# A two-block transformer step on one core: deferred uses of turned tiles, and token-major state-space channels

## The chip, the cores and the metric

The program runs on one core of one Trainium2 chip. The time is the device time of one launch in microseconds (us); three runs of the kernel before gave 1686.46, 1687.34 and 1688.99 us, median 1687.34.

## The reference, cut to what matters

256 tokens of width 1024 go through two blocks. The first block has two layers. Each layer is a feed-forward network (SwiGLU), a mixer, and a second feed-forward network. The second block has one mixer of another kind, one cross-attention and one feed-forward network, which the change reaches only through the feed-forward network's helper. The mixer of a layer of the first block is

```python
uv, c_q, c_kv, k_rope, z, xbc, dt_raw, gates = jnp.split(h @ w_in[l], IN_OFFSETS, axis=-1)
y_a = gmlp_mixer(uv, ...)                      # gelu, norm, a 128x128 matrix over tokens, product
y_b = mla_mixer(c_q, c_kv, k_rope, ...)        # low-rank heads, rope, causal attention
y_c = ssd_mixer(z, xbc, dt_raw, ...)           # xbc: causal conv of width 4 over tokens, silu, then the scan
g = jax.nn.sigmoid(gates).reshape(bsz, s, N_BRANCH, D_MODEL)
merged = (g[:, :, 0] * (y_a @ w_branch[l, 0]) + g[:, :, 1] * (y_b @ w_branch[l, 1])
          + g[:, :, 2] * (y_c @ w_branch[l, 2]))
x = x + merged @ w_out[l]
```

`xbc` has 1024 channels: 512 are the scan's inputs, 512 its two state projections. The convolution runs along tokens, one channel at a time.

## The kernel before, in words

**Products.** All weights are float32. `wload` (L158) brings a tile of 128x1024 weights from memory into a ring `stage` of 5, ScalarE casts it to the ring `whi` of 4 (L165), and VectorE writes the rest of the split, `wlo`, also 4 deep (L166). Each product of 128 x 128 x n is then three matmuls, high by high, high by low and low by high (`mac`, L288; they show as L290, L291 and L292). With 512 columns a weight tile holds two of the eight 128-row pieces of the width, and both 128-token tiles use it: 2 x 2 x 3 = 12 matmuls for a tile. The slot of weight tile i is free again when the last matmul of tile i-4 is done.

**Two directions.** `lin_tok` (L294) gives token-major results: activations are the stationary operand, 512 weight columns the moving one. `lin_ft` (L313) gives channel-major results (channels on partitions): 128 weight columns are stationary, and the 256 tokens move. The mixer's `xbc` uses `lin_ft`, since the convolution wants tokens along the free axis.

**Turning a tile.** A token-major result that feeds a product has to be turned. `to_T` (L258) does it with TensorE transposes into PSUM, then `split_evac` (L187: a cast on ScalarE, a subtraction on VectorE). `flip_T` (L282) does it without TensorE: `flip` (L267) has VectorE transpose 32x32 blocks into a tile `flip` (L273), SyncE writes it to memory `flips` in four pieces (L277), and reads it back as `flipped` (L279); `split_evac` follows. The channels then stand in another order, so the weight rows behind are permuted on the host (`_flipped`). `flipped` has one buffer.

**Order.** The mixer's steps come in the order of a list,

```python
SEQ = "x u q z S A g0 b0 g2 g1 b2 b1"
```

x: the state-space channels and their convolution; u: the gated MLP up to its turned output `yaT`; q: heads; z: the state-space gate; S: the scan, output `ycT`; A: attention, output `ybT`; g0, g1, g2: gate projections; b0, b1, b2: the branch products of `yaT`, `ybT`, `ycT`. After the last branch the merged rows `mg` are transposed to `mh`, `ml` for the product with `w_out`. Within these, the tile framework fixes each engine's order of instructions when the program is built, by priorities (weights and the chains S and A stand higher) and by what its own schedule has ready; on the chip each engine then works through its list in that order. SyncE issues all transfers, weights and turned tiles alike, from one list.

Of the kernel before, what the change touches and what calls it, by code (L numbers as in the profile page):

```python
# [16 lines left out]
P = 128  # L17
# [14 lines left out]
BUFS = dict(  # L32
    sg=2, hb=1, flip=2, flipped=1,
    cg=2, xb=2, gv=2, gu=2, sq=2, q=2, k=2, kv=4, xs=2, xd=2, y=2, yo=2, jk=2, pr=2, pT0=2, pT1=2, ao=2, L=2, cbm=2, rp=2,
    D1=2, Mb=2, pm=2, XT=2, X=3, s5m0=2, s5x0=2, s5t=4, sq2=2, tg=1, o2=1, vn=2)
SEQ = "x u q z S A g0 b0 g2 g1 b2 b1"
NS, NW = 5, 4
COLS = ((0, 512), (512, 512))
LAST = ((0, 512), (512, 256), (768, 256))
# [27 lines left out]
class Net:  # L67
    def __init__(self, ctx, tc, a, outs):
        self.tc, self.nc, self.a, self.outs = tc, tc.nc, a, outs
        mk = lambda n, b=None, **k: ctx.enter_context(tc.tile_pool(name=n, bufs=b, **k))  # L70
        self.big = mk("big")
        self.sma, self.small = None, {}
        self.junk = mk("junk", 1)
        self.ps = mk("ps", space=PSUM)
        self.dram = mk("dram", 2, space=bass.MemoryType.DRAM)
        self.lane = ""
        self.wdma, self.ahead = [], []
# [73 lines left out]
    def _shape(t, shape):  # L151
# [4 lines left out]
        return t.rearrange("p (a b c) -> p a b c", b=shape[1], c=shape[2])  # L156

    def wload(self, src, shape):  # L158
        nc = self.nc
        n = int(np.prod(shape))  # L160
        i = len(self.wdma)
        with self.tc.high_priority(WPRIO):
            s, h, l = [ring[:, i % ring.shape[1], :n] for ring in (self.stage, self.whi, self.wlo)]
            self.wdma.append(self.dma(s, src, 4))
            nc.scalar.copy(h, s)  # L165
            self.wsub = nc.vector.tensor_tensor(l, s, h.bitcast(F32), ALU.subtract).ins  # L166
        return self._shape(h, shape), self._shape(l, shape)
# [98 lines left out]

    def flip(self, src, w, rows=4):  # L267


        nc = self.nc  # L270
        n = rows * w
        r = self.A([512], "flip")[:, :n]
        nc.vector.transpose(r, src)  # L273
        d = self.dram.tile([P, 512], F32, name="flips", tag="flips")[:32 * rows, :4 * w]
        to = d.rearrange("(j c) (i e) -> i c j e", c=32, e=w)
        for i in range(4):
            nc.sync.dma_start(out=to[i], in_=r[i * 32:i * 32 + 32].rearrange("p (j e) -> p j e", e=w))  # L277
        raw = self.A([512], "flipped")[:32 * rows, :4 * w]
        nc.sync.dma_start(out=raw, in_=d)  # L279
        return raw.rearrange("p (a k b) -> p a k b", a=4, b=32)  # L280

    def flip_T(self, src, n, hi, lo, t):  # L282

        tok = slice(t * P, (t + 1) * P)
        hi, lo = [z[:, :, tok].rearrange("p k (a b) -> p k a b", b=32) for z in (hi, lo)]
        self.split_evac(self.flip(src, n * 32).rearrange("p a k b -> p k a b"), hi, lo)

# [25 lines left out]
    def lin_ft(self, xT, w, c, out):  # L313
# [186 lines left out]
    def mixer1(self, l, norm, nxt):  # L500
        nc, a = self.nc, self.a
        v, act, pe = nc.vector, nc.scalar, nc.tensor
        tt, stt, ts = v.tensor_tensor, v.scalar_tensor_tensor, v.tensor_scalar
        lay = self.lay = Arena(self, 3072, "lay1")
        xT, r = norm["xT"], norm["r"]
# [58 lines left out]

        xc, qkv, zs = [], [], []

        def channels():

            rrow = self.r_rows(r, lay)
            for g in range(2):  # L570
                xb = self.A([4, S], "xb")
                for c2 in range(2):
                    p = self.mm()
                    for c in range(2):
                        self.lin_ft(xT, self.wcols(a["m1_xbc"][l][g * 4 + c2 * 2 + c][None], P), 0, p[:, c * S:(c + 1) * S])
                    tt(xb[:, c2 * 2:c2 * 2 + 2], self._shape(p, [2, S]),
                       rrow[:, None, :].to_broadcast([P, 2, S]), ALU.mult)
                d = self.A([4, S], "xc")
# [22 lines left out]
        def heads():  # L601
# [3 lines left out]
            for hf in range(2):  # L605
# [4 lines left out]
                for t in range(2):  # L610
                    p, pk = pqs[t], pks[t]
                    with self.tc.high_priority(EPRIO):
# [47 lines left out]
        def ssd():  # L660
# [18 lines left out]
            for t in range(2):  # L679
# [134 lines left out]
        for step in SEQ.split():  # L814
            i = int(step[1:] or 0)
            if step[0] == "b":
                branch(i, ys[i], not begun)
# [676 lines left out]
def _prep(inp):  # L1494
# [117 lines left out]
```

## Time and profile before

| | us |
|---|---|
| median of 3 runs | 1687.34 |
| the profiled execution's own time | 1684.87 |
| its span, first to last instruction | 1683.2 |
| TensorE busy in it | 1653.3 (98%) |
| VectorE busy | 1152.4 (68%) |
| ScalarE busy | 904.5 (54%) |
| mean granted TensorE clock | 0.996 of 2.4 GHz |

Matmuls are pipelined: one of 512 columns lasts 391 ns by itself, and the next starts long before it ends. What one costs is the distance between two starts, so the timeline is the view to read it from, not the busy time. The mixer of layer one runs from about 196 to 416 us, that of layer two from about 799 to 1018 us.

### The profile page before, as it was taken

How to read it: one execution, taken by the hardware profiler on the slowest of the kernel's cores; microseconds unless marked ns; L12 is line 12 of the kernel's file. 1: busy time of each engine (PE TensorE's matmuls, PEld its weight loads, DVE VectorE, ACT ScalarE, POOL GpSimd, SP SyncE). 2: the span in 40 equal slices, each digit the busy share in tenths (PEclk: the TensorE clock that was granted, in tenths of full speed). 3: DMA queues.
4: the chain of work that ended last, by engine and by line, in shares of the span. 5: the costliest groups of instructions: out<-in, count | busy, mean ns of one | idle time of the engine just before them, and what ended most of it. 6: DMA issues, size and time to landing. Idle time of an engine off the chain costs nothing.

```text
span 1683.2 us, 24727 instructions
## 1 busy us (share of the span) xinstructions
PE 1653.3 (98%) x9090; PEld 1412.7 (84%) x9090; DVE 1152.4 (68%) x1904; ACT 904.5 (54%) x1361; POOL 80.7 (5%) x73
## 2 busy tenths in 40 slices
PE   8999999998999999999999989999999999999998
PEld 6888898887888888888988877888899888888888
DVE  5665599756666556665897666799689746756664
ACT  5444476663545444444676645545477555654443
POOL 0000013000000000000121000000010100000000
PEclk9999999999999999999999999999999999999999
DMA  7777577753687757776777645767764224347872
GB/s 258 242 239 246 178 225 235 225 179 122 193 252 249 230 176 237 248 242 184 230 232 232 191 147 188 225 211 235 230 196 144 64 63 154 123 151 246 260 234 98
DMA packets 158986, 337.15 MB, mean 200 GB/s; under 512 B 35984, under 2 KB 76432, under 8 KB 158864
## 3 DMA queue, kind: packets, MB, share of 16 engines
q1 hardware_dynamic: 158864, 335.57, 63.6%
q8 instruction: 71, 1.16, 0.3%
q14 instruction: 51, 0.42, 0.1%
HBM read 312.43 MB, written 23.07 MB: 199 GB/s over the span
## 4 chain that ended last, share of the span: by engine, by line
PE 95%; DVE 1%; ACT 1%; DMA 1%; issue 0%; SPq 0%; POOL 0%; POOLq 0%; DVEq 0%; ACTq 0%
PE mm L290 28%; PE mm L291 28%; PE mm L292 28%; PE tp L206 1%; PE mmm L290 1%; PE mmm L292 1%; PE mmm L291 1%; PE ch L758 1%; PE chs L1005 1%; PE ch L780 1%; PE ch L1143 0%; PE ch L721 0%; ACT whi L165 0%; PE tp L773 0%; PE ch L1138 0%
## 5 line engine op out<-in xcount | busy, mean ns | idle before, releaser
L166 DVE TENSOR_TENSOR wlo<-stage,whi 128x1024 fp32r<-128x1024 f32 (+3 forms) x552 | 659.6, 1199 | 331.6 <-ACT whi L165 313.1
L165 ACT CAST whi<-stage 128x1024 fp32r<-128x1024 f32 (+3 forms) x552 | 568.4, 1035 | 445.1 <-PE mm L292 366.0
L291 PE MATMUL mm<-wlo,xh 128*128 128x512 f32 (+3 forms) x1264 | 484.2, 385 | 0.0
L292 PE MATMUL mm<-whi,xl 128*128 128x512 f32 (+4 forms) x1264 | 481.0, 385 | 0.0
L290 PE MATMUL mm<-whi,xh 128*128 128x512 f32 (+3 forms) x1264 | 468.1, 385 | 0.1
L291 PEld LDWEIGHTS mm<-wlo,xh 128*128 128x128 f32 x1264 | 237.8, 188 | 45.7 <-DVE wlo L166 0.2
L290 PEld LDWEIGHTS mm<-whi,xh 128*128 128x128 f32 x1264 | 237.0, 188 | 45.9 <-ACT xh L210 0.5
L292 PEld LDWEIGHTS mm<-whi,xl 128*128 128x128 f32 x1264 | 236.8, 188 | 44.8
L292 PE MATMUL mm<-whi,hTl 128*128 128x512 f32 (+1 forms) x484 | 179.0, 370 | 0.0
L291 PE MATMUL mm<-wlo,hTh 128*128 128x512 f32 (+1 forms) x484 | 179.0, 370 | 0.0
L290 PE MATMUL mm<-whi,hTh 128*128 128x512 f32 (+1 forms) x484 | 178.8, 371 | 0.0
L174 POOL TENSOR_TENSOR small<-small,cst 128x1 f32<-128x1 f32 (+2 forms) x60 | 62.1, 1043 | 1154.1 <-DVE small L172 1110.1
L188 ACT CAST hTh<-flipped 128x512 fp32r<-128x512 f32 (+1 forms) x60 | 35.2, 587 | 132.5 <-DMA flipped<-flips 130.9
L292 PEld LDWEIGHTS mm<-whi,hTl 128*128 128x128 f32 x484 | 91.2, 188 | 15.5
L290 PEld LDWEIGHTS mm<-whi,hTh 128*128 128x128 f32 x484 | 91.2, 189 | 15.3
L291 PEld LDWEIGHTS mm<-wlo,hTh 128*128 128x128 f32 x484 | 91.3, 189 | 15.2
L189 DVE TENSOR_TENSOR hTl<-flipped,hTh 128x512 fp32r<-128x512 f32 (+1 forms) x60 | 38.8, 647 | 79.5 <-ACT hTh L188 75.3
L291 PE MATMUL mm<-xl,whi 128*128 128x256 f32 x320 | 90.7, 284 | 1.1 <-DVE xl L211 1.1
L290 PE MATMUL mm<-xh,whi 128*128 128x256 f32 x320 | 90.3, 284 | 1.2 <-ACT xh L210 1.2
L292 PE MATMUL mm<-xh,wlo 128*128 128x256 f32 x320 | 90.2, 283 | 0.0
L291 PEld LDWEIGHTS mm<-xl,whi 128*128 128x128 f32 x320 | 61.3, 192 | 1.6 <-DVE xl L211 1.5
L290 PEld LDWEIGHTS mm<-xh,whi 128*128 128x128 f32 x320 | 61.2, 192 | 1.4 <-ACT xh L210 1.4
(519 smaller groups left out, 2004.2 us busy)
## 6 DMA issues: line engine op xcount, KB each, us to landing
stage<-in_ffn_in SPq DMA_DIRECT2D x176, 512.0 KB, 4.3
stage<-in_ffn_out SPq DMA_DIRECT2D x88, 512.0 KB, 4.4
stage<-in_m_g SPq DMA_DIRECT2D x48, 512.0 KB, 4.6
stage<-in_f_in SPq DMA_DIRECT2D x44, 512.0 KB, 4.4
flips<-flip SPq DMA_DIRECT2D x232, 64.0 KB, 3.2
flipped<-flips SPq DMA_DIRECT2D x58, 256.0 KB, 3.6
stage<-in_m_br SPq DMA_DIRECT2D x24, 512.0 KB, 4.6
stage<-in_m_out SPq DMA_DIRECT2D x24, 512.0 KB, 3.6
```

Of the source, the lines that this page charges most:

```text
L165: nc.scalar.copy(h, s)
L166: self.wsub = nc.vector.tensor_tensor(l, s, h.bitcast(F32), ALU.subtract).ins
L174: nc.gpsimd.tensor_tensor(r, m, self.mhalf[:, :n], ALU.pow)
L188: self.nc.scalar.copy(hi, ps)
L189: self.nc.vector.tensor_tensor(lo, ps, hi.bitcast(F32), ALU.subtract)
L206: nc.tensor.transpose(p[:, k, t * P:(t + 1) * P], x[t][:, (k0 + k) * P:(k0 + k + 1) * P], self.ident)
L290: mm(out, lh, rh, start=first, stop=False)
L291: mm(out, lh, rl, start=False, stop=False)
L292: mm(out, ll, rh, start=False, stop=last)
L758: pe.matmul(p3[:, i], qT[:96, b * hb + i, toks[t]], kT[:96, b * hb + i, :nk], start=True, stop=True)
L780: pe.matmul(p[:, h * 64:(h + 1) * 64], pT[kb][:, h], vv[kb][:, h], start=kb == 0, stop=kb == t)
L1005: pe.matmul(q, self.s5bc[ct][:, 2 * (E5 - 1 - e) + i], um[:, :, e], start=e == 0, stop=e == E5 - 1)
```

## The change

There are four parts.

1. **Deferred uses.** `flip` no longer reads back at once. It puts two things on a list: the read of `flipped`, due 5 weight tiles later or more, and the use (the ScalarE cast and what follows), due 3 weight tiles after that. `wload` runs what is due before it loads the next tile, and orders it behind the last weight tile's transfer and cast. `flipped` has two buffers. `FLUSH` names steps in front of which what an earlier step has put on the list is run at once: b0 flushes u's, A flushes q's, q flushes what stands ahead of the steps, c flushes x's. All feed-forward networks use `flip_T` and so follow the new rule.
2. **Channels.** `xbc` is projected token-major with 512 columns (`lin_flip`), scaled on ScalarE, turned by `flip`, and copied by ScalarE into `xb`. The row of scales across channels (`r_rows`, two transposes) and the scaling on VectorE (four instructions of 128x512 a mixer) go. The convolution is a step of its own, c.
3. **Attention and scan outputs** are turned by `to_T` instead of `flip_T`: 2 x 4 transposes for `ycT` and 4 x 2 for `ybT` a mixer.
4. **Order.** z comes before q, S before g0, A behind g0.

```diff
+FLUSH = dict(q="k", c="x", A="q", b0="u")
-SEQ = "x u q z S A g0 b0 g2 g1 b2 b1"
+SEQ = "x z q c u S g0 A b0 g2 g1 b2 b1"
 NS, NW = 5, 4
+FLIPS = 5, 3
...
+    def later(self, n, fn):
+        self.seq += 1
+        self.due.append((n, self.seq, self.step, fn))
+    def run_due(self, n):
+        while self.due and min(self.due)[0] <= n:
+            d = min(self.due)
+            self.due.remove(d)
+            with self.tc.issue_after(self.wdma[-1]), self.tc.issue_after(self.wcast):
+                d[3]()
+    def flush(self, step):
+        self.run_due(max([d[0] for d in self.due if d[2] == step], default=0))
...
     def wload(self, src, shape):
+        if self.due:
+            self.run_due(len(self.wdma))
...
-    def flip(self, src, w, rows=4):
+    def flip(self, src, w, use, rows=4):
...
-        raw = self.A([512], "flipped")[:32 * rows, :4 * w]
-        nc.sync.dma_start(out=raw, in_=d)
-        return raw.rearrange("p (a k b) -> p a k b", a=4, b=32)
+        at = max(len(self.wdma) + FLIPS[0], min(self.frees) + 1)
+        self.frees.remove(min(self.frees))
+        self.frees.append(at + FLIPS[1])
+        box = []
+        def load():
+            box.append(self.A([512], "flipped")[:32 * rows, :4 * w])
+            nc.sync.dma_start(out=box[0], in_=d)
+        self.later(at, load)
+        self.later(at + FLIPS[1], lambda: use(box[0].rearrange("p (a k b) -> p a k b", a=4, b=32)))
...
+    def lin_flip(self, xT, src, out, r=None):
+        act = self.nc.scalar
+        ps = self.lin_tok(xT, src, 512)
+        for t in range(2):
+            z = self.A([512], "hb")
+            if r:
+                act.activation(z, ps[t], AF.Copy, scale=r[t])
+            else:
+                act.copy(z, ps[t])
+            to = out[:, :, t * P:(t + 1) * P].rearrange("p k (a b) -> p k a b", b=32)
+            self.flip(z, P, lambda raw, to=to: act.copy(to, raw.rearrange("p a k b -> p k a b")))
...
-            rrow = self.r_rows(r, lay)
             for g in range(2):
                 xb = self.A([4, S], "xb")
-                for c2 in range(2):
-                    p = self.mm()
-                    for c in range(2):
-                        self.lin_ft(xT, self.wcols(a["m1_xbc"][l][g * 4 + c2 * 2 + c][None], P), 0, p[:, c * S:(c + 1) * S])
-                    tt(xb[:, c2 * 2:c2 * 2 + 2], self._shape(p, [2, S]),
-                       rrow[:, None, :].to_broadcast([P, 2, S]), ALU.mult)
+                self.lin_flip(xT, a["m1_xbc"][l][g * 4:g * 4 + 4], xb, r)
+                xbs.append(xb)
...
-                self.flip_T(y, 4, ycT[0], ycT[1], t)
+                self.to_T(y, 4, ycT[0], ycT[1], t)
...
-                    self.flip_T(o.rearrange("p a b -> p (a b)"), 2, ybT[0][:, hf * 2:hf * 2 + 2],
+                    self.to_T(o.rearrange("p a b -> p (a b)"), 2, ybT[0][:, hf * 2:hf * 2 + 2],
...
+            if step in FLUSH:
+                self.flush(FLUSH[step])
+            self.step = step
```

On the host the columns of `xbc` and the rows of the branch weights are permuted to suit. What follows shows how three places of the first mixer are laid out; the second mixer has the same three. Line numbers of the changed kernel differ: L320 to L322 are the three matmuls (L290 to L292 before), L519 the row broadcast (L476), L763 the scan's product (L721), L738 its state product (L696), L637 the gated MLP's matrix over tokens (L595), L284 a `to_T` transpose (L263), L295 the VectorE turn (L273).

TensorE before, where the scan S and the branch product b0 meet: `ch<-cst,small` is a row broadcast from which ScalarE makes the scan's decay matrices L, and `ch<-xd,L`, 45 rows further down, is the product that reads them.

```order
L292 MATMUL mm<-whi,yaT 128x512
L696 MATMUL ch<-xdd,bt 128x256 x2
L476 MATMUL ch<-cst,small 128x128 x4
L290 MATMUL mm<-whi,yaT 128x512
L476 MATMUL ch<-cst,small 128x128 x4
L291 MATMUL mm<-wlo,yaT 128x512
L292 MATMUL mm<-whi,yaT 128x512
L290 MATMUL mm<-whi,yaT 128x512
L291 MATMUL mm<-wlo,yaT 128x512
L292 MATMUL mm<-whi,yaT 128x512
```

TensorE now, at the end of the gate projection g0 (`mm<-...,xh` or `xl`) and the start of b0 (`mm<-...,yaT`).

```order
L321 MATMUL mm<-wlo,xh 128x512
L322 MATMUL mm<-whi,xl 128x512
L637 MATMUL ch<-gv,lay_1422 128x128
L738 MATMUL ch<-xdd,bt 128x256 x2
L637 MATMUL ch<-gv,lay_1422 128x128 x3
L519 MATMUL ch<-cst,small 128x128 x8
L763 MATMUL ch<-xd,L 128x64 x4
L519 MATMUL ch<-cst,small 128x128 x8
L763 MATMUL ch<-xd,L 128x64 x4
L320 MATMUL mm<-whi,yaT 128x512
L321 MATMUL mm<-wlo,yaT 128x512
L322 MATMUL mm<-whi,yaT 128x512
```

Before, broadcasts and products of the scan had matmuls of b0 and g0 between them. Now all of g0 stands ahead of the first broadcast, b0 behind the last product of the first token tile, and nothing but the scan and the gated MLP's second half in between.

VectorE before, around the turn of the gated MLP's two tiles (`flip<-gu`); `L469` and the like are the small softplus steps, `wlo` is a weight tile.

```order
L166 TENSOR_TENSOR wlo<-stage,whi 128x768
L469 TENSOR_SCALAR small<-small 128x16
L598 SCALAR_TENSOR_TENSOR gu<-ch,lay_1422,gu 128x128 x4
L468 TENSOR_TENSOR small<-small 128x16
L598 SCALAR_TENSOR_TENSOR gu<-ch,lay_1422,gu 128x128 x4
L273 STREAM_TRANSPOSE flip<-gu 128x512
L469 TENSOR_SCALAR small<-small 128x16
L273 STREAM_TRANSPOSE flip<-gu 128x512
L166 TENSOR_TENSOR wlo<-stage,whi 128x768
```

VectorE now, around the same turn; `L<-L,cbm` is the product that finishes the scan's decay matrices, the two `wlo` are the last two weight tiles of b0.

```order
L187 TENSOR_TENSOR wlo<-stage,whi 128x1024 x2
L295 STREAM_TRANSPOSE flip<-q 128x384
L640 SCALAR_TENSOR_TENSOR gu<-ch,lay_1422,gu 128x128 x4
L295 STREAM_TRANSPOSE flip<-k 128x384
L759 TENSOR_TENSOR L<-L,cbm 128x512 x2
L295 STREAM_TRANSPOSE flip<-gu 128x512 x2
L766 TENSOR_TENSOR y<-y,ch 128x512
L775 SCALAR_TENSOR_TENSOR y<-y,small,z 128x512
L193 TENSOR_SCALAR small<-small 128x2
L210 TENSOR_TENSOR yaT<-flipped,yaT 128x4x128
```

The turn has moved from behind the gated MLP's own products (`gu<-ch`) to behind the scan's decay matrices.

TensorE before, at the end of attention: `ch<-kv,pT` are attention's last products, `mm<-...,ybT` is b1, `tp<-cst,mg` and `mh`, `ml` belong to the product with `w_out`.

```order
L780 MATMUL ch<-kv,pT_2803 128x64
L291 MATMUL mm<-wlo,ybT 128x512
L292 MATMUL mm<-whi,ybT 128x512
L263 MATMUL tp<-cst,mg 128x128 x4
L290 MATMUL mm<-whi,mh 128x512
L291 MATMUL mm<-wlo,mh 128x512
L263 MATMUL tp<-cst,mg 128x128 x4
L292 MATMUL mm<-whi,ml 128x512
L290 MATMUL mm<-whi,mh 128x512
L291 MATMUL mm<-wlo,mh 128x512
L292 MATMUL mm<-whi,ml 128x512
L290 MATMUL mm<-whi,ybT 128x512
```

TensorE now, where the last attention tile `ao` is transposed.

```order
L322 MATMUL mm<-whi,ycT 128x512
L320 MATMUL mm<-whi,ybT 128x512
L321 MATMUL mm<-wlo,ybT 128x512
L322 MATMUL mm<-whi,ybT 128x512
L320 MATMUL mm<-whi,ybT 128x512
L321 MATMUL mm<-wlo,ybT 128x512
L284 MATMUL tp<-cst,ao 128x128 x2
L322 MATMUL mm<-whi,ybT 128x512
L320 MATMUL mm<-whi,ybT 128x512
L321 MATMUL mm<-wlo,ybT 128x512
```

Before, twelve matmuls of b1 stood behind the first matmuls of `w_out`. Now the transposes of `ao` stand behind the first five of the 48 matmuls of b1, and the other 43 follow before the first transpose of `mg`.

## Rows read from the trace of the kernel before

**Rows 1.** The page: busy time of the span and instructions of each engine.

```profile
PE 1653.3 (98%) x9090; PEld 1412.7 (84%) x9090; DVE 1152.4 (68%) x1904; ACT 904.5 (54%) x1361; POOL 80.7 (5%) x73
```

**Rows 2.** Waits of TensorE: who for whom, us in total, times, longest us.

```profile
PE mm L290 <- ACT ybT L188: 7.5, 2, 4.4
```

**Rows 3.** TensorE's timeline, first mixer's end: start us, us, what, [idle before <-releaser].

```profile
397.37 0.60 PE L263 MATMUL tp<-cst,mg 128*128 128x128 f32 x4
...
404.08 0.79 PE L290 MATMUL mm<-whi,ybT 128*128 128x512 f32 x1 [3.04 <-ACT ybT L188]
...
412.06 0.39 PE L292 MATMUL mm<-whi,ml 128*128 128x512 f32 x1
```

**Rows 4.** TensorE's timeline, second mixer's end.

```profile
999.34 0.60 PE L263 MATMUL tp<-cst,mg 128*128 128x128 f32 x4
...
1007.43 0.74 PE L290 MATMUL mm<-whi,ybT 128*128 128x512 f32 x1 [4.42 <-ACT ybT L188]
...
1015.04 0.40 PE L290 MATMUL mm<-whi,mh 128*128 128x512 f32 x1
```

**Rows 5.** Windows: stretch, us, busy PE, PEld, DVE, ACT, POOL (instructions), PEclk, DMA, GB/s.

```profile
409.00:410.00 1.00, 1.00 (x5) 0.67 (x4) 0.71 (x2) 0.40 (x1) 0.00 (x0) 0.50 0.00 0
```

**Rows 6.** VectorE, SyncE and ScalarE timelines, the last attention tile of mixer one.

```profile
398.18 0.44 DVE L273 STREAM_TRANSPOSE flip<-ao 128x256 f32<-128x256 f32 x1
...
398.64 1.75 SPq L277 DMA_DIRECT2D flips<-flip  x4
...
403.62 0.40 ACT L188 CAST ybT<-flipped 128x256 fp32r<-128x256 f32 x1 [3.10 <-DMA flipped<-flips]
```

**Rows 7.** TensorE's timeline, matmuls of 256 columns, then of 512.

```profile
214.17 0.28 PE L291 MATMUL mm<-xl,whi 128*128 128x256 f32 x1
...
218.97 0.28 PE L292 MATMUL mm<-xh,wlo 128*128 128x256 f32 x1
...
312.14 0.39 PE L291 MATMUL mm<-wlo,yaT 128*128 128x512 f32 x1
...
318.04 0.39 PE L290 MATMUL mm<-whi,xh 128*128 128x512 f32 x1
```

**Rows 8.** TensorE's timeline, four transposes between matmuls.

```profile
302.82 0.60 PE L683 MATMUL tp<-cst,xc 128*128 128x128 f32 x4
303.18 0.48 PE L291 MATMUL mm<-wlo,yaT 128*128 128x512 f32 x1
```

**Rows 9.** TensorE's timeline, the state-space scan of mixer one.

```profile
307.40 1.02 PE L696 MATMUL ch<-xdd,bt 128*128 128x256 f32 x4
308.26 0.60 PE L476 MATMUL ch<-cst,small 128*128 128x128 f32 x4
...
319.03 2.11 PE L721 MATMUL ch<-xd,L 128*128 128x64 f32 x16
320.97 1.04 PE L476 MATMUL ch<-cst,small 128*128 128x128 f32 x8
```

**Rows 10.** The chain in order of time, gated-MLP matmuls: start us, us, what.

```profile
254.72 1.78 PE ch L595 x16
```

**Rows 11.** ScalarE's timeline, table load and decay matrices of the scan.

```profile
297.53 1.28 ACT L677 ACT_TABLE_LOAD   x1
298.83 0.21 ACT L677 ACTIVATE small<-small 128x8 f32<-128x8 f32 x1
...
313.83 2.15 ACT L715 ACTIVATE L<-ch,small 128x128 f32<-128x128 f32 x8
...
318.24 0.63 ACT L716 ACTIVATE L<-L 128x512 f32<-128x512 f32 x1
```

**Rows 12.** VectorE's timeline, turn of a gated-MLP tile, and a decay product.

```profile
258.38 0.70 DVE L273 STREAM_TRANSPOSE flip<-gu 128x512 f32<-128x512 f32 x1
...
319.29 0.69 DVE L717 TENSOR_TENSOR L<-L,cbm 128x512 f32<-128x512 f32 x1
```

**Rows 13.** Windows, heads and gated MLP of mixer one (columns as in rows 5).

```profile
280.00:290.00 10.00, 10.00 (x46) 8.29 (x45) 10.00 (x32) 5.24 (x8) 4.98 (x3) 1.00 0.73 208
```

More of the change, by code (lines that the diff above doesn't have):

```diff
@@ L76, in __init__ @@
         self.lane = ""
-        self.wdma, self.ahead = [], []
+        self.wdma, self.ahead, self.due, self.frees, self.step, self.seq = [], [], [], [0] * BUFS["flipped"], None, 0
         self.sma = Arena(self, 1536, "small")
@@ L164, in wload @@
             self.wdma.append(self.dma(s, src, 4))
-            nc.scalar.copy(h, s)
+            self.wcast = nc.scalar.copy(h, s).ins
             self.wsub = nc.vector.tensor_tensor(l, s, h.bitcast(F32), ALU.subtract).ins
@@ L273, in flip @@
         nc.vector.transpose(r, src)
-        d = self.dram.tile([P, 512], F32, name="flips", tag="flips")[:32 * rows, :4 * w]
+        d = self.dram.tile([P, 512], F32, name="flips", tag="flips", bufs=12)[:32 * rows, :4 * w]
         to = d.rearrange("(j c) (i e) -> i c j e", c=32, e=w)
@@ L285, in flip_T @@
         hi, lo = [z[:, :, tok].rearrange("p k (a b) -> p k a b", b=32) for z in (hi, lo)]
-        self.split_evac(self.flip(src, n * 32).rearrange("p a k b -> p k a b"), hi, lo)
+        self.flip(src, n * 32, lambda raw: self.split_evac(raw.rearrange("p a k b -> p k a b"), hi, lo))
     def mac(self, out, lh, ll, rh, rl, first, last):
@@ L503, in mixer1 @@
         tt, stt, ts = v.tensor_tensor, v.scalar_tensor_tensor, v.tensor_scalar
-        lay = self.lay = Arena(self, 3072, "lay1")
+        lay = self.lay = Arena(self, 2560, "lay1")
         xT, r = norm["xT"], norm["r"]
@@ L538, in mixer1 @@
             rh.append(h)
+        self.step = "k"
         pas = self.lin_tok(xT, a["m1_cq"][l], 384)
@@ L563, in mixer1, with convolved @@
             kpe.append(k_)
-        xc, qkv, zs = [], [], []
+        xc, xbs, qkv, zs = [], [], [], []
         def channels():
-            rrow = self.r_rows(r, lay)
             for g in range(2):
                 xb = self.A([4, S], "xb")
-                for c2 in range(2):
-                    p = self.mm()
-                    for c in range(2):
-                        self.lin_ft(xT, self.wcols(a["m1_xbc"][l][g * 4 + c2 * 2 + c][None], P), 0, p[:, c * S:(c + 1) * S])
-                    tt(xb[:, c2 * 2:c2 * 2 + 2], self._shape(p, [2, S]),
-                       rrow[:, None, :].to_broadcast([P, 2, S]), ALU.mult)
+                self.lin_flip(xT, a["m1_xbc"][l][g * 4:g * 4 + 4], xb, r)
+                xbs.append(xb)
+        def convolved():
+            for g, xb in enumerate(xbs):
                 d = self.A([4, S], "xc")
@@ L640, in heads @@
                         for src, dst in ((q3, qT), (kk, kT)):
-                            z = self.flip(src.rearrange("p b h c -> p (b h c)"), P, 3)
-                            act.copy(dst[:96, :, toks[t]].rearrange("p h (a b) -> p h a b", b=32),
-                                     z.rearrange("p a h b -> p h a b"))
+                            to = dst[:96, :, toks[t]].rearrange("p h (a b) -> p h a b", b=32)
+                            self.flip(src.rearrange("p b h c -> p (b h c)"), P,
+                                      lambda z, to=to: act.copy(to, z.rearrange("p a h b -> p h a b")), 3)
                 qkv.append((qT, kT, vv, sc))
@@ L824, in mixer1 @@
             else:
-                dict(x=channels, u=gmlp, q=heads, z=ssd_gate)[step]()
+                dict(x=channels, c=convolved, u=gmlp, q=heads, z=ssd_gate)[step]()
         mh = [self.A([4, S], "mh", F32R) for _ in range(2)]
@@ L1473, with _flipped_to @@
 HID = (512,) * 5 + (256,)
+def _flipped_to(w):
+    return w.reshape(w.shape[0], -1, 4, 4, 32).transpose(0, 1, 3, 2, 4).reshape(w.shape)
 def _out_w(w, cols=COLS):
@@ L1509, in _prep @@
     cqw, ckvw, xbc, zz, uv, gg, uq, ukv, br = [], [], [], [], [], [], [], [], []
-    ways = (512,), (256, 256), (512,)
+    ways = (512,), (128,) * 4, (128,) * 4
     for l in range(2):
@@ L1514, in _prep @@
         ckvw.append(_blk(np.concatenate([wl[:, 1408:1696], wl[:, 3232:3240]], axis=1), 0, 296, 2))
-        xbc.append(np.concatenate([_blk(wl, 2208 + P * i, P, 8) for i in range(8)]))
+        xbc.append(np.concatenate([_blk(_flipped_to(wl[:, 2208:3232]), 512 * i, 512, 2) for i in range(2)]))
         zz.append(_blk(wl, 1696, 512, 2))
```

2 lines of the change are left out of this document (1 added, 1 removed).

## The prediction

> **What bounds the kernel now.** I read the page first, then who TensorE waits for, then its timeline where it waits. The page shows TensorE busy for 98% of the span [rows 1]; that figure alone would let one think that only shorter products can help. TensorE idles some 30 us in all. Outside the start and the end of the program the waits of TensorE have one large entry, the turned attention tile `ybT`, 7.5 us in two waits, one for each mixer [rows 2]. In the feed-forward networks TensorE waits for nothing, so whatever the new rule for turned tiles does there, there is no idle time to win.
>
> At the end of the first mixer TensorE needs 14.69 us from the first transposes of `mg` at 397.37 to the even flow at 412.06 [rows 3]. In it the timeline has 22 matmuls of 512 columns and 12 transposes. Even flow is 0.227 us a matmul (26 starts in 5.90 us) [rows 7] and 0.09 us a transpose (four in 0.36) [rows 8]: 5.0 + 1.1 = 6.1 us. So 8.6 us are lost there. Only 3.04 of them are the wait itself; behind it the granted clock is 0.50, the lower level of 1.2 GHz, and it is still there in the stretch from 409 to 410 us, over five us after the wait [rows 5]. The second mixer needs 15.70 us for 23 matmuls and 12 transposes, 6.3 us of work: 9.4 us lost [rows 4]. Together 18.0 us. Why it waits is in rows 6: VectorE turns the last `ao` at 398.18, SyncE writes it at 398.64, and ScalarE casts what came back only at 403.62.
>
> **The change part by part.**
>
> *The end of attention.* With `to_T` the last `ao` tile needs two transposes (0.18), a cast and a subtraction, under 2 us in all, and 43 matmuls of b1 follow (9.8 us), 20 of them before the first that reads this tile. The wait goes, and with it the slow clock. What is late next is the end of `mg`: behind the last matmul of b1 VectorE has two steps of about 0.69 [rows 12] for each of the two tiles, then transposes, casts and subtractions, with only a few matmuls of `w_out` as cover. I put this at 2 us a mixer, as in the small waits that stand there now. Gain 18.0 - 4 = 14 us; bounds 11 and 18.
>
> *The start of b0.* This is the place that decides. Now u stands late, g0 is used up before the scan's broadcasts, and the branch b0 waits for `yaT`. Let T0 be the end of the last g0 matmul. The weight ring holds b0's four tiles then, so no other tile can serve as filler; TensorE's list has only the scan and the rest of the gated MLP: four matmuls over tokens 0.89 (half of eight in 1.78 [rows 10]), two state products 0.86, eight scan products 1.94 [rows 9], 16 broadcasts at 0.09, together 5.1 us. Everything that `yaT` needs hangs in a row behind these. To the eighth broadcast: 0.89 + 0.86 + 0.72 = 2.5 us. ScalarE: eight Relu steps 2.15, a table load with 1.30 to the next start, two Exp 1.2 [rows 11]. VectorE: the last L product 0.69, and only then the turn of `gu` 0.70 [rows 12], since VectorE takes its list in order. That is T0 + 8.5. From the end of a turn to the matmul took 404.08 - 398.62 = 5.5 us in the first mixer [rows 3, 6], and in the second the wait was 1.4 longer [rows 4]. SyncE's list puts three further transfers (one read of a head tile, two pieces of the second `gu`) ahead of the read, at 0.44 each (four in 1.75 [rows 6]): 1.3. The first `yaT` matmul starts at T0 + 15.3 to 16.7, and TensorE idles 10 to 11.5 us. I take 10.5. Behind it I expect the lower clock, as behind the shorter wait of rows 3: nearly six us at half speed cost 2.9 there; I take 2.5. So 13 us a mixer, 26 us. Bounds: if the table load and SyncE's three transfers are hidden, 7.6 of idle and 1.5 of clock, 18 us; if ScalarE reaches the Relu steps 1.5 us late, since the last cast, a gate and two copies stand ahead of them, 16 a mixer, 32 us.
>
> The load of the Exp table is in the chain because the gated MLP's gelu now comes between the scan's two uses of Exp. Rows 11 show the load at 297.53 and the next activation at 298.83. The Trainium skill (ScalarE: Activation LUTs, What ACT_TABLE_LOAD costs) puts a switch at a load of about 1283 ns and a drain of about 1380 ns besides. By that rule the chain would be 1.4 us longer and the estimate of the whole 1704; the trace agrees with the load and shows no drain, so the row decides.
>
> *The wider projection.* Before, 192 matmuls of 256 columns a mixer at 0.120 us (40 starts in 4.80 [rows 7]), 23.0 us; now 96 of 512 at 0.227, 21.8 us: 1.25 us less, 2.5 for both. The two broadcasts of `r_rows` go: 0.4 for both. The transposes of `to_T` come, 16 a mixer at 0.09: 2.9 us for both. Net 0, at most 1 us more for switching between the kinds. The Trainium skill (TensorE: Matmul & The Clock Gate, Wait — 56ns, not 53.3ns?) has starts of warm matmuls N / 2.4 GHz plus some 2.5 ns apart. By that rule the wide form would save only 0.2 us a mixer and the whole come to 1703; the rows show 120 and 227 ns, so the trace does not agree, and the rows stand.
>
> *VectorE.* A mixer loses four scalings of 128x512, the turns of two `y` (0.70) and four `ao` (0.44 [rows 6]), and gets four turns of `xbc` (0.70); that is less work, not more. But the convolution now lies in the same stretch as the heads' and the gated MLP's work. By an estimate from durations of before, VectorE's list from the last heads tile to the last b0 tile comes to about 56 us, against 55 for TensorE's. Before, VectorE was busy 10.00 of 10 us in such a stretch while TensorE was too [rows 13]. I take 1 us a mixer; bounds 0 and 3. If that cover is gone, each weight tile waits for its `wlo`.
>
> *Deferred uses in the feed-forward networks.* A use comes 8 weight tiles after its turn, 8 x 12 x 0.227 = 21.8 us; the last pair is read in the 11th tile of the output product. SyncE no longer holds weights behind a read. TensorE had no wait there, so nothing is won; nothing is lost while three tiles (8 us) of margin remain. Zero.
>
> Sum: -14 + 26 + 0 + 2 = +14 us on the profiled execution's own 1684.87, 1698.9. The median of the runs, 1687.34, is 2.5 above it, so I forecast 1701 us.
>
> **The rivals.**
>
> *The wait at b0 is short, and the kernel is faster.* SyncE has few weight transfers there, so the turned tile could come back sooner than in rows 6, and with a short wait the clock would stay up. The point is 7 us a mixer, half of what the end gains: the first `yaT` matmul before T0 + 12, at full clock. At 5 us each the sum is -18 + 10 = -8, 1679 us. Against it: in rows 3 and 6 hardly any weights were in flight either, and the chain up to the turn alone takes 8.5 us.
>
> *VectorE becomes the bound from q to g0.* For it: its list is as long as TensorE's. Against it: rows 13. At 10% more than summed it is 5.6 us late, 11 us for both instead of 2: 1710 us.
>
> *Deferred uses come late in the feed-forward networks.* There are five networks; 3 us at each output product would give 15: 1716 us. For it: the uses queue behind weight casts on ScalarE. Against it: the margin above.
>
> **How the numbers follow.** Forecast 0.77, the wait at b0 short 0.09, VectorE 0.09, feed-forward 0.05. The forecast's own bounds reach from 1687 (18 lost, 18 gained) to 1714 (32 lost, 11 gained, 6 for VectorE); its corners are unlikely, so 1690 to 1714 holds eight in ten with VectorE's case in it. A measurement of this kernel tells 0.2%, some 3.4 us, from no change. Faster by more than that takes the first rival: 0.09. Within it, the forecast's lowest corner or a milder first rival: 0.05. Slower: 0.86.
>
> **What would show it.** In the profile after, TensorE's largest wait should be `mm<-whi,yaT` behind the cast of `yaT`, twice, about 10 us each with the scan's matmuls just before it, and a granted clock of 0.50 behind it. The waits for `ybT` should be gone. VectorE's turn of `gu` should follow the L products by no idle time. The `xbc` matmuls should start 0.227 us apart. I am wrong if TensorE waits under 5 us there, if the waits for `ybT` stay, or if TensorE waits in the feed-forward networks.

## The result and the profile after

The changed kernel takes 1716.11 us (median of four runs, 1715.07 to 1718.43), against 1687.46 us before (four runs of the same job): ratio 1.0171, 95% interval [1.0153, 1.0188]. It is 28.7 us slower. I had forecast 1701, with a range to 1714. The direction was right, the size was not. The profiled executions, 1715.07 and 1684.87, lie 30.2 apart.

The page has TensorE busy for 97% of a longer span, 98% before [rows 1]:

```profile
PE 1661.8 (97%) x8926; PEld 1410.8 (82%) x8926; DVE 1147.4 (67%) x1892; ACT 918.0 (54%) x1377; POOL 81.4 (5%) x73
```

The waits of TensorE (who for whom, total, times, longest) have lost `ybT` [rows 2] and have two new entries:

```profile
PE ch L763 <- DVE L L759: 11.7, 2, 6.2
PE mm L320 <- ACT yaT L209: 11.5, 2, 6.0
```

TensorE's timeline shows where that is. First comes a mark at the start of each mixer and at the end of the second, then the stretch around b0 of the first, and the same places in the second:

```profile
193.18 0.33 PE L320 MATMUL mm<-whi,xh 128*128 128x384 f32 x1
...
811.00 0.33 PE L320 MATMUL mm<-whi,xh 128*128 128x384 f32 x1
...
1065.60 0.39 PE L322 MATMUL mm<-whi,ml 128*128 128x512 f32 x1
```

```profile
302.16 0.38 PE L637 MATMUL ch<-gv,lay 128*128 128x128 f32 x2
...
303.91 1.04 PE L519 MATMUL ch<-cst,small 128*128 128x128 f32 x8
311.14 1.97 PE L763 MATMUL ch<-xd,L 128*128 128x64 f32 x8 [6.19 <-DVE L L759]
312.90 1.91 PE L519 MATMUL ch<-cst,small 128*128 128x128 f32 x8
...
322.44 0.79 PE L320 MATMUL mm<-whi,yaT 128*128 128x512 f32 x1 [6.03 <-ACT yaT L209]
...
327.73 0.40 PE L284 MATMUL tp<-cst,y 128*128 128x128 f32 x2
...
920.69 0.38 PE L637 MATMUL ch<-gv,lay 128*128 128x128 f32 x2
...
939.73 0.79 PE L320 MATMUL mm<-whi,yaT 128*128 128x512 f32 x1 [5.44 <-ACT yaT L209]
...
945.02 0.63 PE L284 MATMUL tp<-cst,y 128*128 128x128 f32 x2
```

Before, the three marks stand at 193.06, 795.65 and 1035.57. So the kernels are level at the first mark, 15.35 us apart at the second and 30.03 at the third; behind it nothing is added (the spans are 30.1 apart). The feed-forward networks between the mixers take 362.9 us in both kernels, from the end of one mixer's `w_out` to the next mixer. All the loss is in the two mixers. A mixer, from its first 384-column matmul to its last of `w_out`, took 239.7 and 239.9 us; now 255.0 and 254.6. The experiments below are read by the sum of the two, 479.6 before and 509.6 now, since the program behind the mixers takes 648 to 654 us in the profiled executions, and 660 in run 5, without a reason that I found.

T0, the end of g0, is 302.16 here, and the first `yaT` matmul starts at T0 + 20.3; in the second mixer (920.69, 939.73) at T0 + 19.0. The granted clock is the last number but two of a window (start and end of it, its length, then the engines' busy time):

```profile
317.00:321.00 4.00, 0.00 (x0) 0.00 (x0) 0.89 (x2) 3.63 (x12) 0.00 (x0) 0.50 0.63 156
323.00:327.00 4.00, 4.00 (x11) 3.05 (x10) 1.60 (x4) 0.62 (x1) 0.00 (x0) 0.50 0.20 66
330.00:334.00 4.00, 4.00 (x19) 3.29 (x18) 3.07 (x6) 0.13 (x1) 0.00 (x0) 1.00 0.00 0
```

TensorE idled, the clock is at its lower level, 1.2 GHz, and stays there for the first 12 matmuls of b0: 5.29 us from 322.44 to 327.73, and as long from 939.73 to 945.02, where 2.7 would do.

Why `yaT` comes at 322 is in the lists of ScalarE, VectorE and SyncE:

```profile
305.26 0.62 ACT L685 COPY qT<-flipped 96x512 f32<-96x512 f32 x1 [1.03 <-DMA flipped<-flips]
305.79 0.58 ACT L740 COPY st<-ch 128x512 f32<-128x512 f32 x1
306.27 2.15 ACT L757 ACTIVATE L<-ch,small 128x128 f32<-128x128 f32 x8
308.44 1.28 ACT L758 ACT_TABLE_LOAD   x1
309.73 1.15 ACT L758 ACTIVATE L<-L 128x512 f32<-128x512 f32 x2
...
321.77 0.62 ACT L209 CAST yaT<-flipped 128x512 fp32r<-128x512 f32 x1 [0.74 <-DMA flipped<-flips]
```

```profile
310.39 1.29 DVE L759 TENSOR_TENSOR L<-L,cbm 128x512 f32<-128x512 f32 x2 [3.50 <-ACT L L758]
311.60 1.30 DVE L295 STREAM_TRANSPOSE flip<-gu 128x512 f32<-128x512 f32 x2
```

```profile
308.52 0.34 SPq L307 DMA_DIRECT2D flipped<-flips  x1
308.95 4.77 SPq L299 DMA_DIRECT2D flips<-flip  x8
313.88 0.32 SPq L307 DMA_DIRECT2D flipped<-flips  x1
314.24 0.43 SPq L299 DMA_DIRECT2D flips<-flip  x1
315.01 0.31 SPq L307 DMA_DIRECT2D flipped<-flips  x1
315.37 2.39 SPq L299 DMA_DIRECT2D flips<-flip  x5
318.78 0.34 SPq L307 DMA_DIRECT2D flipped<-flips  x1
```

The first `gu` is turned at 312.25 (half of the 1.30). SyncE is then still writing eight pieces of head tiles; behind them stands a read (313.88), then one piece of `gu`, then another read, which waits until its tile's pieces have landed (315.01), and only then the other pieces. The read of `gu` goes out at 318.78. How long SyncE stood at its reads until the pieces of their tiles had landed is in its own list of waits; from 300 to 323 us that was 5.8 us in six waits, the longest 2.7, ahead of the read at 308.52:

```profile
SPq L307 <- DMA flips<-flip: 5.8, 6, 2.7
```

From turn to matmul it took 10.2 us; before, 5.5 [rows 3, 6]. The read of that tile, which rows 6 leave out, went out at 401.64:

```profile
401.64 0.34 SPq L279 DMA_DIRECT2D flipped<-flips  x1
```

At the end of the mixer, which answers to rows 3, 5.1 us go by from the first transposes of `mg` at 420.64 to 425.78, with 12 transposes and three matmuls in them, 1.8 us of work:

```profile
420.64 0.60 PE L284 MATMUL tp<-cst,mg 128*128 128x128 f32 x4
422.43 0.50 PE L320 MATMUL mm<-whi,mh 128*128 128x512 f32 x1 [1.19 <-ACT mh L209]
...
423.71 1.09 PE L284 MATMUL tp<-cst,mg 128*128 128x128 f32 x8 [0.55 <-DVE mg L853]
425.45 0.50 PE L322 MATMUL mm<-whi,ml 128*128 128x512 f32 x1 [0.64 <-DVE ml L210]
```

So 3.4 us are lost there instead of 8.6; the second mixer has the same three waits (1.18, 0.64, 0.58).

### The profile page after: what moved, and what is told of

Its sections match the earlier page's. It is cut to its first block, busy times and chain, and to the rows that moved or that the text cites. A ratio compares the mean times of both kernels' runs of the same rounds, so it can differ in the third digit from the quotient of the medians.

```text
span 1713.3 us, 24434 instructions
## 1 busy us (share of the span) xinstructions
PE 1661.8 (97%) x8926; PEld 1410.8 (82%) x8926; DVE 1147.4 (67%) x1892; ACT 918.0 (54%) x1377; POOL 81.4 (5%) x73
## 4 chain that ended last, share of the span: by engine, by line
PE 85%; DVE 6%; DMA 3%; ACT 2%; issue 2%; SPq 1%; POOL 0%; POOLq 0%; ACTq 0%; DVEq 0%
PE mm L320 25%; PE mm L322 25%; PE mm L321 25%; DVE wlo L187 2%; DMA flips<-flip 1%; DMA flipped<-flips 1%; PE tp L227 1%; DVE xc L531 1%; ACT whi L186 1%; PE mmm L320 1%; PE mmm L322 1%; SPq L299 1%; PE mmm L321 1%; PE ch L800 1%; PE chs L1050 1%
## 5 line engine op out<-in xcount | busy, mean ns | idle before, releaser
L321 PE MATMUL mm<-wlo,xh 128*128 128x512 f32 (+3 forms) x1328 | 508.6, 385 | 0.0
L322 PE MATMUL mm<-whi,xl 128*128 128x512 f32 (+3 forms) x1328 | 506.8, 386 | 0.0
L320 PE MATMUL mm<-whi,xh 128*128 128x512 f32 (+3 forms) x1328 | 491.8, 386 | 3.3 <-ACT whi L186 3.2
L320 PEld LDWEIGHTS mm<-whi,xh 128*128 128x128 f32 x1328 | 248.9, 188 | 54.0 <-ACT whi L186 6.3
L322 PEld LDWEIGHTS mm<-whi,xl 128*128 128x128 f32 x1328 | 248.8, 188 | 47.5
L322 PE MATMUL mm<-whi,hTl 128*128 128x512 f32 (+1 forms) x484 | 179.0, 370 | 0.0
L320 PE MATMUL mm<-whi,hTh 128*128 128x512 f32 (+1 forms) x484 | 178.9, 371 | 0.0
L322 PEld LDWEIGHTS mm<-whi,hTl 128*128 128x128 f32 x484 | 91.2, 189 | 15.4
L320 PEld LDWEIGHTS mm<-whi,hTh 128*128 128x128 f32 x484 | 91.2, 189 | 15.3
L209 ACT CAST hTh<-flipped 128x512 fp32r<-128x512 f32 (+1 forms) x60 | 34.6, 581 | 77.5 <-DMA flipped<-flips 76.3
L321 PE MATMUL mm<-xl,whi 128*128 128x256 f32 x192 | 54.5, 285 | 1.1 <-DVE xl L232 1.1
L320 PE MATMUL mm<-xh,whi 128*128 128x256 f32 x192 | 54.1, 284 | 1.2 <-ACT xh L231 1.2
L322 PE MATMUL mm<-xh,wlo 128*128 128x256 f32 x192 | 54.0, 283 | 0.0
L295 DVE STREAM_TRANSPOSE flip<-hb 128x512 f32<-128x512 f32 (+1 forms) x68 | 45.6, 670 | 1.6
L431 ACT ACTIVATE sg<-mm,small 128x512 f32<-128x512 f32 (+1 forms) x60 | 39.1, 651 | 8.7 <-PE mm L322 8.6
```

The lines of the kernel that those rows point to most:

```text
L209: self.nc.scalar.copy(hi, ps)
L320: mm(out, lh, rh, start=first, stop=False)
L321: mm(out, lh, rl, start=False, stop=False)
L322: mm(out, ll, rh, start=False, stop=last)
L431: nc.scalar.activation(sg[:, :n], pg[t][:, :n], AF.Silu, scale=r[t])
```

## The experiments

The theory: the loss is one hole in TensorE's list at b0, made by the place of u in the order; SyncE's list sets how long it is. The rivals are named with each run. "Before" is run beside each, 1685.1 to 1685.8 us.

**1. Fill the hole.** g2 goes ahead of b0.

```diff
-SEQ = "x z q c u S g0 A b0 g2 g1 b2 b1"
+SEQ = "x z q c u S g0 A g2 b0 g1 b2 b1"
```

> The changed kernel with the gate projection g2 ahead of b0 in the order (x z q c u S g0 A g2 b0 g1 b2 b1), so that 96 matmuls that need neither the scan nor yaT stand where TensorE idled. Theory (the whole loss is the hole at b0): both waits there go, the granted clock stays at 1.00, some 17 us a mixer come back: 1716 - 34 = 1682 us, below the kernel before. Rival (deferred uses or the wide projection cost time elsewhere): half or less comes back, 1700 or more.

1685.08 us, ratio to before 0.9996 [0.9986, 1.0005]; the mixers together 475.0, 34.6 less than in the changed kernel. Both waits are gone. So filler work at b0 gives back more than the 30 us that the change lost. Not all of it is the hole at b0: the waits at the end of `mg` are gone as well (none over 0.5 us there).

**2. Move u alone.**

```diff
-SEQ = "x z q c u S g0 A b0 g2 g1 b2 b1"
+SEQ = "x u z q c S g0 A b0 g2 g1 b2 b1"
```

> The changed kernel, all four parts, with one step moved: u stands ahead of z and q instead of behind c (x u z q c S g0 A b0 g2 g1 b2 b1), so that 51 matmuls of the gate projection stand between the scan's broadcasts and the products, and yaT is turned long before b0. Theory (the loss is the hole at b0, made by the late u; S before g0 and A behind it cost nothing): both waits go, 31 to 35 us come back, 1682 us, and against part 3 alone (1677.6) some 5 us of turned tiles in the heads stay. Rival (the scan ahead of g0 makes the loss wherever u stands): 1700 or more.

1677.89 us, ratio 0.9949 [0.9935, 0.9962], 38 us below the changed kernel with all four parts in it; the mixers 469.4. TensorE's timeline has 51 other matmuls, 11.6 us, between the first broadcasts and the products, and no wait at either place (nor one over 0.3 us at the end of `mg`):

```profile
289.23 1.04 PE L519 MATMUL ch<-cst,small 128*128 128x128 f32 x8
...
301.71 1.00 PE L763 MATMUL ch<-xd,L 128*128 128x64 f32 x8
```

So with u early the other parts, S ahead of g0, A behind it, the wide projection and the deferred uses, cost nothing against part 3 alone (run 9), and gain nothing over it either. In the old order the wide projection and the deferred uses do cost time (runs 10 and 11). The theory's guess that 5 us of turned tiles would stay was wrong.

**3. Shorten the chain up to the turn.** Tanh for gelu, so that no table load is left in the chain.

```diff
-                act.activation(gv, pvs[t], AF.Gelu, scale=r[t])
+                act.activation(gv, pvs[t], AF.Tanh, scale=r[t])
-                act.activation(u, pus[t], AF.Gelu, scale=r[t])
+                act.activation(u, pus[t], AF.Tanh, scale=r[t])
```

> The changed kernel with tanh in the place of gelu in the gated MLP (the output differs by that), so that no table load stands between the scan's Relu and Exp. Theory A (the chain of the prediction: everything up to the matmul in a row): both the decay matrices and the first yaT matmul come 1.3 us sooner in each mixer, 1716 - 2.6 = 1713.4 us. Theory B (SyncE's list, not the turn of gu, sets when yaT comes): the wait for the decay matrices shrinks by 1.3, the first yaT matmul comes less than 0.5 sooner, 1715.5 us.

1715.66 us, ratio 1.0177 [1.0161, 1.0193]. SyncE's list stands at nearly the same times as in the changed kernel (its eight pieces of head tiles begin at 309.12, there at 308.95). Against it the turn comes 1.3 us sooner, the first piece of `gu` and the matmul don't (VectorE, SyncE, TensorE):

```profile
310.29 1.30 DVE L295 STREAM_TRANSPOSE flip<-gu 128x512 f32<-128x512 f32 x2
```

```profile
314.38 0.43 SPq L299 DMA_DIRECT2D flips<-flip  x1
```

```profile
322.43 0.80 PE L320 MATMUL mm<-whi,yaT 128*128 128x512 f32 x1 [7.33 <-ACT yaT L209]
```

The piece now goes out 3.4 us behind the turn instead of 2.0, and the time is theory B's. The run is less clean than its edit: T0 is 300.56 here, 1.6 us earlier, and counted from T0 the turn isn't sooner, since ScalarE waits 2.00 us at a head copy instead of 1.03, and the matmul comes 1.6 us later. In the second mixer `L` comes 0.75 us sooner from T0 and the matmul 0.5 later. So a sooner `L` or turn alone brought the matmul no sooner; it follows SyncE's list.

**4. Shorten SyncE's list.** The last head tiles aren't turned.

```diff
                         for src, dst in ((q3, qT), (kk, kT)):
+                            if hf == 1 and t == 1:
+                                nc.gpsimd.memset(dst[:96, :, toks[t]], 0.0)
+                                continue
```

> The changed kernel without the turns of the last head tiles (second half of the heads, second token tile; q and k are set to zero there), which takes eight write pieces and two reads a mixer out of SyncE's list, right ahead of the pieces of gu. Theory B (SyncE's list sets when yaT comes): the first yaT matmul comes 3 us or more sooner in each mixer, 1709 us. Theory A (the turn's chain sets it, SyncE's pieces cost 1.3 as predicted): 1.3 sooner, 1713.4.

1702.04 us, ratio 1.0105 [1.0087, 1.0122]; the mixers 494.0, 15.6 less. From the first broadcasts to `yaT` 14.5 and 12.7 us instead of 18.5 and 17.3:

```profile
302.26 1.04 PE L519 MATMUL ch<-cst,small 128*128 128x128 f32 x8
...
316.71 0.79 PE L320 MATMUL mm<-whi,yaT 128*128 128x512 f32 x1 [2.60 <-ACT yaT L209]
```

That is more than theory B gave, but the edit did more than take pieces away. VectorE's list changed too, and the first `gu` is turned ahead of `L`, at T0 + 2.4 instead of T0 + 9.4 (T0 is 300.51 here):

```profile
302.93 0.70 DVE L295 STREAM_TRANSPOSE flip<-gu 128x512 f32<-128x512 f32 x1
```

Its first piece still goes out only at 307.21, behind a read of a head tile (306.78), and the matmul comes 4 us sooner from T0, not 7. So here, too, SyncE's list and not the turn sets the hole's length; what each piece less is worth the run can't tell, with two copies fewer on ScalarE in it as well.

**5. Another queue for the reads.**

```diff
-            nc.sync.dma_start(out=box[0], in_=d)
+            nc.gpsimd.dma_start(out=box[0], in_=d)
```

> The changed kernel, with the reads of turned tiles issued from GpSimd's queue instead of SyncE's. Theory (of the 10.2 us from yaT's turn to its first matmul 3.4 are SyncE standing at the reads of two head tiles until their writes have landed): SyncE writes the gu pieces right behind the turn, the first yaT matmul comes 3 us sooner, 1716 - 6 = 1710 us. Rival (the transfers themselves are slow there, the queue is no matter): 10 us from turn to matmul as before, 1716.

1724.50 us, ratio 1.0226 [1.0207, 1.0244]. The mixers took 505.7, 3.9 less; the program behind them, where the edit moves reads too, took 12.8 more, which I can't explain. In the first mixer the turn came at 307.52 already, since the new build has it ahead of `L`, yet the first `yaT` matmul (321.18) came 13 us behind the end of it. SyncE wrote the first `gu`'s pieces right behind the turn, as the theory has it (the last four of the five in the first row, from 309.00). GpSimd then waited for them to land, and ScalarE cast the tile only when it had done the scan's next steps without a pause (SyncE, GpSimd, ScalarE):

```profile
308.60 2.23 SPq L299 DMA_DIRECT2D flips<-flip  x5
```

```profile
316.06 0.57 POOL L307 DMA_DIRECT2D flipped<-flips  x1 [4.60 <-DMA flips<-flip]
```

```profile
320.52 1.12 ACT L209 CAST yaT<-flipped 128x512 fp32r<-128x512 f32 x2
```

So with the reads off its list SyncE was no longer what held the tile up, but the landing of the pieces and ScalarE's list took the time instead, in part as the rival has it. As a price of the reads the run is inconclusive.

**6. Keep TensorE busy.** Dummy matmuls, 44 and 56 a mixer.

```diff
+                if t == 0:
+                    with self.tc.issue_after(last):
+                        for _ in range(N1):
+                            pe.matmul(py[:, :S], xT[0][0][:, :P], xT[0][1], start=True, stop=True)
```

> The changed kernel with 100 matmuls of 256 columns a mixer added whose results nobody reads: 44 behind the first eight broadcasts of the scan, 56 behind its first eight products, where TensorE idles. Theory A (of some 18 us lost there a mixer 6 are the lower clock, and the granted clock falls because TensorE idles): the clock stays at 1.00, about 6 us a mixer come back: 1704 us. Theory B (the clock costs 2.5 us a mixer, as put in the prediction): 1711. Rival (the clock falls whatever TensorE does there): 1716 or more.

1713.68 us, ratio 1.0154 [1.0136, 1.0172]; the mixers 504.0. Neither theory's number: 56 were too many, and `yaT` started 21.8 us behind T0. But with TensorE busy the clock is at its upper level again before `yaT` comes (a window's figure is a mean, so 0.63 is part of it at either level):

```profile
305.00:309.00 4.00, 4.00 (x35) 4.00 (x35) 1.34 (x5) 3.23 (x11) 0.00 (x0) 1.00 0.94 311
...
314.00:318.00 4.00, 4.00 (x25) 4.00 (x25) 1.27 (x3) 3.02 (x8) 0.70 (x1) 0.63 0.73 167
318.00:321.00 3.00, 3.00 (x28) 3.00 (x27) 1.57 (x3) 0.69 (x2) 0.00 (x0) 1.00 0.43 133
324.00:328.00 4.00, 4.00 (x19) 3.30 (x18) 3.88 (x7) 1.87 (x6) 0.00 (x0) 1.00 0.00 0
```

b0 then runs at even flow. So the clock's price is what is slow behind the hole, 2.6 us a mixer in the profile after; slow matmuls inside the hole only wait less. Theory A had counted them. The 5.5 us that came back are no measure of it, since some of the scan's transposes stand ahead of `yaT` here.

**7. Turn yaT on TensorE,** order as changed.

```diff
-                self.flip_T(u, 4, yaT[0], yaT[1], t)
+                self.to_T(u, 4, yaT[0], yaT[1], t)
```

> The changed kernel, order and all, but the gated MLP's output is turned by TensorE transposes (16 more) instead of through memory. Theory (the hole at b0 is there because yaT comes back late; with yaT early, b0's matmuls fill the wait for the decay matrices too): both waits go, 1716 - 34 + 3 for the transposes = 1685 us, as with g2 ahead of b0. Rival (the wait for the decay matrices is its own loss, the order's): only the second wait and half the clock come back, about 9 us a mixer: 1698.

1696.46 us, ratio 1.0062 [1.0047, 1.0077]; the mixers 490.3, 19.3 less. No wait for `L` is left, but a wait of 2.5 us a mixer for `yaT`, still late since u is. Nearer to the rival's number, for another reason than the rival's.

**8. The order alone,** on the kernel before.

```diff
-SEQ = "x u q z S A g0 b0 g2 g1 b2 b1"
+SEQ = "x z q u S g0 A b0 g2 g1 b2 b1"
```

> The kernel before with the new order of steps alone (x z q u S g0 A b0 g2 g1 b2 b1). Theory (the hole at b0 needs the order and the late turn of yaT together): yaT is read back long before b0, 12 of its matmuls stand between the scan's broadcasts and products, so only a wait for the decay matrices of about 3.5 us and some clock is left there, 5 us a mixer, and the attention's end, now with 44 matmuls of b2 behind it, loses 5 a mixer less: 1687 us, between 1682 and 1694. Rival (the order alone makes the loss): TensorE waits over 10 us a mixer at b0, 1705 or more.

1701.10 us, ratio 1.0081 [1.0062, 1.0100]; the mixers 495.9, 16.2 more. I expected no loss; the time is outside the theory's range and nearer the rival's 1705. The loss is in the same stretch, for other tiles of the scan; ScalarE stood 3.7 and 3.8 us at two head copies (295.26 and 301.58) ahead of them. So over half of the 30 us comes with the order alone, in which u is late as well:

```profile
PE ch L696 <- DVE xdd L693: 11.8, 2, 6.1
...
PE mm L290 <- ACT L L715: 4.5, 2, 2.9
```

**9. The transposes alone,** on the kernel before.

```diff
-                self.flip_T(y, 4, ycT[0], ycT[1], t)
+                self.to_T(y, 4, ycT[0], ycT[1], t)
-                    self.flip_T(o.rearrange("p a b -> p (a b)"), 2, ybT[0][:, hf * 2:hf * 2 + 2],
+                    self.to_T(o.rearrange("p a b -> p (a b)"), 2, ybT[0][:, hf * 2:hf * 2 + 2],
```

> The kernel before with part 3 alone: attention and scan outputs turned by TensorE transposes. Theory (the changed kernel gains at the attention's end and loses more at b0): the 18.0 us lost at the two ends of attention in the kernel before fall to about 7.5, as in the changed kernel, and 32 transposes cost 2.9: 1687.5 - 10.5 + 2.9 = 1680 us, and no wait for ybT over 1 us. Rival (the transposes and their switches cost what the wait gives): 1687.

1677.56 us, ratio 0.9952 [0.9937, 0.9966], a little better than the theory; the mixers 471.8. The longest wait for `ybT` is 0.5.

**10. With the wide projection,** read back and used at once.

> The kernel before with part 3 (attention and scan outputs by TensorE transposes) and part 2 (channels token-major with 512 columns, turned, read back at once). Against part 3 alone, 1677.6 us. Theory (width: 1.25 us a mixer less by the starts, two broadcasts less, the rest beside TensorE): 1675 us, between 1673 and 1678. Rival (turned tiles and casts hold up the weights in the heads, as in the changed kernel between 240 and 280 us): 1 to 2 us a mixer more instead, 1680.

1687.91 us, ratio 1.0010 [0.9999, 1.0020]: the rival, and more. The edit is `lin_flip` of the changed kernel in `channels`, with the convolution right behind. ScalarE stands 2.9 us at the read-back and is then busy up to its gelu of `gu`, which is late, and TensorE waits for it 2.4 us, by my reading for the PSUM tile that gelu frees (ScalarE, TensorE):

```profile
246.27 0.62 ACT L333 COPY xb<-flipped 128x512 f32<-128x512 f32 x1 [2.88 <-DMA flipped<-flips]
```

```profile
258.73 0.44 PE L290 MATMUL mm<-whi,cqT 128*128 128x384 f32 x1 [2.36 <-ACT gu L599]
```

**11. With the deferred uses** (part 1 and part 3 only: the changed kernel with the old order and the old channels).

> The kernel before with part 3 and part 1 (deferred uses, two flipped buffers, flushes), old order, channels as before. Against part 3 alone, 1677.6 us. Theory (TensorE waits for nothing in the feed-forward networks, and yaT is flushed long before b0 in the old order): no change, 1677.6 within 3. Rival (deferred uses come late in the feed-forward networks): 3 us in each of five, 1690 or more.

1684.27 us, ratio 0.9989 [0.9977, 1.0002], 6.7 above part 3 alone, between theory and rival, and not in the feed-forward networks (362.9 between the mixers) but in the mixers, 482.3. ScalarE stands 6 us at a deferred head copy, ahead of the scan's Relu, and TensorE then waits for `L` (ScalarE, TensorE):

```profile
315.14 0.62 ACT L687 COPY qT<-flipped 96x512 f32<-96x512 f32 x1 [5.98 <-DMA flipped<-flips]
```

```profile
320.11 1.15 PE L765 MATMUL ch<-xd,L 128*128 128x64 f32 x8 [2.57 <-DVE L L761]
```

**12. Part 3 and heads behind z.**

```diff
-SEQ = "x u q z S A g0 b0 g2 g1 b2 b1"
+SEQ = "x u z q S A g0 b0 g2 g1 b2 b1"
```

> The kernel before with part 3 (attention and scan outputs by TensorE transposes) and the heads moved behind the state-space gate (x u z q S A g0 b0 g2 g1 b2 b1), against part 3 alone, 1677.6 us. Theory (what counts is how much ready work TensorE has behind each chain): the scan now has matmuls of the heads and of g0 beside it and the attention ends with 34 matmuls of b1 behind it, so the 4.6 us lost at each end shrink by 1 to 2: 1675 us, between 1672 and 1678. Rival (the heads' VectorE and ScalarE work beside the scan holds up weights or the decay matrices): 1682 or more.

1677.33 us, ratio 0.9953 [0.9939, 0.9967]. The mixers are the shortest of all, 466.5, 5.3 below part 3 alone, as the theory has it; the program behind them took 3.5 longer than there, so the whole is the same. Runs 2, 9 and 12 beat both kernels and are equal within their intervals.

## Why the prediction was right in direction and wrong in size

- **What bounds the kernel** held: the loss is in the mixers alone, and most of it is TensorE's waits and the slow clock behind them.
- **The start of b0**, 26 us, measured 34.3. The place came as told; the wait there came in two, 6.2 us for `L` and 6.0 for `yaT`, not as one of 10. Of 20.3 and 19.0 us behind T0, 5.1 are work, so 15.2 and 13.9 were lost, not 10.5, and 2.6 a mixer to the clock. **The step that failed is the path from the turn of `gu` to the matmul**, forecast at 6.8 us: 5.5 as in rows 3 and 6, and 1.3 for "three further transfers". It took 10.2 and 9.6 us. The three transfers cost 1.5 and 1.4 there, as priced. What I had left out is that SyncE, which stood at a read of a head tile and then wrote eight pieces, had no room for the first piece of `gu` until 2.0 and 1.6 us behind the turn (0.02 in rows 6), and that from read to matmul a tile of 128x512 took 3.7 and 3.6 us, the `ao` tile of half the size 2.4.
- **The chain up to the turn**, 8.5 us, took 10.1 and 9.4. In the first mixer ScalarE waited 1.0 us for a head tile and did two copies ahead of the Relu steps, about what my upper bound had. It cost little by itself, since SyncE had no room for a sooner turn: in run 3 a sooner `L` brought the matmul no sooner, in run 4 a turn 7 us sooner, with fewer pieces, brought it 4 us.
- **The table load** cost what its row showed: from the first Relu to Exp 3.46 us with it (306.27 to 309.73), 2.02 without it (run 3, 306.37 to 308.39), so 1.44. The Trainium skill (ScalarE: Activation LUTs, What ACT_TABLE_LOAD costs) has a drain of some 1.38 us on top of the load; no such drain is in these rows.
- **The clock** behind the hole, 2.5 us a mixer, measured 2.6.
- **The end of attention**, -14 us, measured -11.2 (18.0 lost before, twice 3.4 now): I had left 2 us a mixer for the end of `mg`.
- **The wide projection and VectorE**, 0 and +2: what is left of the 30.0 is 30.0 - 34.3 + 11.2 = 6.9, a difference and not itself read from rows, 4.9 more than forecast. Waits for `whi`, ScalarE's cast, 3.2 us in seven waits ahead of T0, are part of it; the rest stays open. The 512-column starts are as forecast, 27 in 6.12 us (222.00 to 228.12), 0.227 each.
- **Deferred uses** cost nothing in the feed-forward networks, as told. That they reorder ScalarE's list inside a mixer (run 11) I had not priced.
- **The rivals**: none came. The late deferred uses have the measured number, 1716, by chance: the networks between the mixers take 362.9 us in both kernels. VectorE as the bound would show as waits for `wlo`, and the mixers have none.
- **The range**: its upper end took 32 us lost at b0, 11 gained at the end and 6 for VectorE as the worst. Measured were 34.3, 11.2 and 6.9. No error made up for another; all three terms missed the same way.

What stays open: why the program behind the mixers takes 648 to 660 us between builds, where the rest of the 6.9 us is, and how much of run 4's gain is SyncE's alone.

## What to carry to other kernels

Where engines work through fixed lists, ask of each chain how much ready work the bounding engine has behind it: the same four edits gave +28.7 us with one step late and -7 us with it early. Part 3 alone gave those 7 us, too, so test the parts one by one. A transfer's delay is read from where its queue stands when it is ready, so look at what the queue is doing in that very stretch, not at the length of the transfer in a quiet one. And a tile that comes back through memory stops each in-order engine that takes it too early, ScalarE as much as SyncE.

## What the hardware showed that I had not expected

The same eight pieces took SyncE 4.77 us in the first mixer (308.95) and 3.71 in the second (927.46). Most single pieces took 0.43 us, as in rows 6, though those are of 32 KB and these of 48; one of the first mixer's took 1.51 (312.21), and why isn't shown. In run 6 the clock's mean was 0.63 from 314 to 318 us, over two us behind a wait of only 1.54 us, while TensorE was busy, and 1.00 in the next window.
